# Host layouts for a two-block transformer kernel, with the second block's tokens grouped by residue mod 4

## The chip, the core and the metric

The kernel runs on one core of a Trainium2 chip. The metric is device time in microseconds (us) of one execution; a run's time is that of the core, and three runs of the kernel before gave a median of 3877.02 us. A core has TensorE (PE; its weight loads are shown apart as PEld), VectorE (DVE), ScalarE (ACT), GpSimd (POOL) and SyncE, whose queue (SP) issues every transfer of this kernel.

## What is computed

1024 tokens of width 1024 pass through two different transformer blocks, all in float32. The second block is applied twice (two layers). What matters here:

```python
# block 1
xn = rms_norm(x, norm_g);  proj = xn @ w_in        # q, k, v, z of both mixers
ya = rms_norm(diff_attention(q1, q2, k1, k2, va, lam, t5_bias)) * silu(za)
yb = neighbourhood_attention(qb, kb, vb, na_rpb) * silu(zb)
x  = x + concat(ya, yb) @ w_out
x  = x + sigmoid(x @ w_ple_gate) * (p @ w_ple_proj)
# block 2, two layers
h    = rms_norm(x, g) * (1 + sc1) + sh1;  proj = h @ w_in
o_dil = dilated_attention(q_d, k_d, v_d, positions, slopes)   # 8 heads
o_mla = latent_attention(...)                                 # dense, 8 heads
x = x + gt1 * (concat(o_dil, o_mla) @ w_out)
x = x + gt2 * (relu(h2 @ w_mlp_in) ** 2 @ w_mlp_out)
```

The dilated attention mixes three branches: a token attends to tokens t + j*dil with |j| <= 64 for dil = 1, 4 and 16 (the last covers the whole sequence at stride 16). For dil = 4 the tokens fall into four streams by their residue mod 4, and each stream is an attention among its own 256 tokens.

## The kernel before

A matrix in float32 is split into a rounded high part and the rest, and a product is three matmuls (`mm3`, L181 to L185: L183, L184, L185) of 128 rows by 256 or 512 columns. Activations lie with features on partitions and tokens along the free axis ("a00h" is feature tile 0, first half of the tokens, high part). The instructions of each engine are put in order by a scheduler that works on a model of the timeline, so an edit in one place can shift the order in others. PE, DVE, ACT, POOL and SP each run their own list in order.

**Start.** `load_x` (L331) loads x by rows in tiles of 128 tokens, transposes them on PE (64 transposes, L155), splits them with the norm's gain into a..h and a..l (ACT L130, DVE L131), copies the raw transposed x (DVE L345) and stores it to `xTd[0]`, and sums squares from the rows (ACT L350). Small vectors are brought onto partitions by `columns` (L164): load as rows, transpose on PE (L169), copy. `consts1` (L271) builds the table of the relative bias of the differential attention by matmul, through DRAM copies `t5d` and `t5s`; `consts2` (L316) builds a skewed copy `rpbs` of the neighbourhood bias in DRAM, eight transfers from DRAM to DRAM. `mod_start` (L930) brings `b_mod`, the norm gains and c.

**Block 1.** Four units of differential attention and four of neighbourhood attention follow; `start` in `diff_groups` (L500) loads the bias tile from `t5s` and `t5d`, `start` in `na_groups` (L615) loads `edge` from `rpbs` by two transfers of 64 partitions x 14 x 64 elements, and POOL adds a mask to it (L624). `put_mix` (L755) transposes an output to features on partitions. `ple_steps` (L359) loads p by rows and transposes it.

**Dilated stage.** For each of four pairs of heads, `stacks` (L424) transposes k and q, splits them and copies them by transfers into `ks0`, `ks1`, `qs0`, `qs1` (128 partitions x 1024 tokens: one head's high and low part); a half of the tokens at a time. `dil_groups` (L1299) then runs eight groups of scores per pair: for each head m first the near branch (x = 0), two groups of four query tiles, then the far branch (x = 1), two groups of four tiles. Each tile of scores is two matmuls (`score`, L459 with `ks`, L460 with `kl`) with 128 queries as weights and 256 keys as the moving operand. The far branch takes queries and keys of one residue by a stride of four tokens:

```python
# L1338, x == 1: stream cc, query tile u
q, ks = slice(cc + 512 * u, cc + 512 * u + 509, 4), slice(cc, cc + 1021, 4)
self.score(ps[:, k % 2, o:o + n], m, q, ks)
# L1369: the stream's output goes back with a stride of four
nc.scalar.copy(c["oTc"].rearrange("p (i c) -> p c i", c=4)[...], ...)
```

That makes 2 layers x 4 pairs x 2 heads x 2 groups x 4 tiles = 128 far tiles, and 128 near ones (96 of them 256 keys wide, in whole). DVE takes each tile from PSUM with a table of distances (`add_min`, L492 to L494), ACT applies the exponential (L1347), PE transposes and multiplies by v, which `scores` loads from DRAM: `v0` for the near branch, `v1` by four transfers for the far one.

**End.** In the last layer `mlp` (L1719) finishes with 16 products of 12 matmuls, each added to x on DVE (L1831); then `store_out` (L1889) transposes x back to rows on PE (64 transposes, L155), copies it out of PSUM (L1901, L1903) and stores it. The scheduler puts many of these transposes between the last products.

Of the kernel before, what the change touches and what calls it, by code (L numbers as in the profile page):

```python
# [15 lines left out]
OP = mybir.AluOpType  # L16
# [13 lines left out]


def shape_constants():
    rel = np.arange(-1023, 1024)
    n = np.abs(rel)
    large = 8 + np.searchsorted(np.array(T5_EDGES), n, side="right")
    bucket = np.where(rel > 0, 16, 0) + np.where(n < 8, n, np.minimum(large, 15))
    onehot = np.zeros((32, 2048), np.float32)
    onehot[bucket, np.arange(2047)] = 1.0
# [6 lines left out]
    wmask = np.where(np.abs(j - 64 - p) <= 64, 0.0, BIG).astype(np.float32)  # L45
# [7 lines left out]
    for cc in range(4):  # L53
        ec[np.arange(P), cc, cc + 4 * (np.arange(P) % 32)] = 1.0
    inv = np.float32(10000.0) ** (-np.arange(16, dtype=np.float32) / np.float32(16))
    return {"c_onehot": onehot, "c_colmask": colmask, "c_wmask": wmask, "c_cmult": cmult,
            "c_ec": np.concatenate([ec.reshape(P, 512), rmask], 1), "c_inv": inv.reshape(1, 16)}

# [28 lines left out]
class Emit:  # L87
# [76 lines left out]
    def columns(self, dst, src, n):  # L164
        nc = self.nc
        t = self.tmp.tile([P, P], F32, tag="colsrc", name="colsrc")
        self.dma(t[:n], src)
        ps = self.psum_t()
        nc.tensor.transpose(ps[:, :n], t[:n], self.ident[:n, :n])  # L169
        nc.vector.tensor_copy(dst, ps[:, :n])  # L170

# [61 lines left out]
    def setup(self):  # L233
# [23 lines left out]
        self.xTd = [self.dram.tile([8, P, S], F32, name=f"xTd{b}") for b in range(3)]  # L257
# [3 lines left out]
    def consts0(self):  # L261
        nc, A, c = self.nc, self.A, self.const
        self.gcol = c.tile([P, 8], F32, name="gcol")
        self.columns(self.gcol, A["norm_g"].rearrange("o (k p) -> (o k) p", p=P), 8)
        self.rs = c.tile([P, 8], F32, name="rs")
        self.hrs = c.tile([P, 8], F32, name="hrs")
        self.ev = c.tile([P, 8], F32, name="ev")
        self.xss = c.tile([P, 2, 8], F32, name="xss")
        self.xvar = c.tile([P, 8], F32, name="xvar")

    def consts1(self):  # L271
        nc, A, c = self.nc, self.A, self.const
        v = self.tmp.tile([P, P], F32, tag="colsrc", name="gsrc")
        for i, n in enumerate(("q_norm_a", "k_norm_a", "q_norm_b", "k_norm_b")):
            for j in range(2):
                self.dma(v[i:i + 1, j * 64:j * 64 + 64], A[n])
        ps = self.psum_t()
        nc.tensor.transpose(ps[:, :4], v[:4], self.ident[:4, :4])
        g4 = c.tile([P, 4], F32, name="g4")
        nc.vector.tensor_copy(g4, ps[:, :4])  # L280
        self.gq = c.tile([P, 2], F32, name="gqk")
        for i in range(2):
            nc.vector.scalar_tensor_tensor(self.gq[:, i:i + 1], g4[:, 2 * i:2 * i + 1], -0.125, g4[:, 2 * i + 1:2 * i + 2],
                                           op0=OP.mult, op1=OP.mult)
        tb = self.tmp.tile([32, 4], F32, name="t5b")
        self.dma(tb, A["t5_bias"])
        self.t5d = self.dram.tile([4, 2048], F32, name="t5d")
        for i in range(4):
            oh = self.tmp.tile([32, 512], F32, tag="onehot", name="onehot")
            self.dma(oh, A["c_onehot"][:, i * 512:(i + 1) * 512])  # L290
            row = self.tmp.tile([4, 512], F32, tag="t5row", name="t5row")
            ps = self.psum_t()
            nc.tensor.matmul(ps[:4], tb, oh, start=True, stop=True)
            nc.scalar.activation(row, ps[:4], AF.Copy, scale=-1.0)
            self.dma(self.t5d[:, i * 512:(i + 1) * 512], row)
        self.t5s = self.dram.tile([4, P, 520], F32, name="t5s")
        for i in range(4):
            t = self.t5s[i]
# [1667 lines left out]
```

## Time and profile before

| | |
|---|---|
| runs | 3874.85, 3877.02, 3882.91 us (median 3877.02) |
| profiled execution | 3880.11 us |
| its span, first to last instruction | 3878.2 us |
| mean granted TensorE clock | 0.973 of full speed |
| PE busy | 3613.2 us (93%) |
| PEld busy | 3097.2 us (80%) |
| DVE busy | 2821.6 us (73%) |
| ACT busy | 1842.2 us (48%) |
| POOL busy | 1565.9 us (40%) |
| chain that ended last | PE 59%, DVE 16%, POOL 8%, DMA 8%, issue 5%, ACT 4% |
| transfers | 446.17 MB, 36.7% of 16 DMA engines |

Busy times overlap across engines. A matmul's duration in the trace includes the filling and draining of the pipeline, so that matmuls overlap on PE; what one matmul costs is read from the time between its start and the start of the next one.

### The profile page before, as it was taken

Reading aid. Unit: us, or ns where it says so; the run is one execution under the profiler, and the core shown is the slowest. Engines: PE = TensorE matmul, PEld = TensorE weight load, DVE = VectorE, ACT = ScalarE, POOL = GpSimd, SP = SyncE. Lnnn points to the kernel's source line nnn. Section 1 sums busy time; section 2 is a strip of 40 time slices with the busy share of each in tenths; the row PEclk is TensorE's granted clock in tenths of the full one; section 3 lists DMA queues with packets and bytes.
Section 4 is the critical chain, followed back from the end, with each engine's and each line's share of the span. In section 5 each row is a group of like instructions: output and inputs, shape, how many; then the busy total and the mean of one; then the engine's idle time right before and its main releaser. Section 6 shows DMA issues by size and latency. Waiting matters only on the chain.

```text
span 3878.2 us, 59074 instructions
## 1 busy us (share of the span) xinstructions
PE 3613.2 (93%) x20508; PEld 3097.2 (80%) x20508; DVE 2821.6 (73%) x6304; ACT 1842.2 (48%) x3671; POOL 1565.9 (40%) x1317
## 2 busy tenths in 40 slices
PE   7999899989899899988998999899899998998999
PEld 6988899768899888777786777899788776886777
DVE  5888877667666788658889986666788646447885
ACT  4555555623455678533333333455677633333331
POOL 2334222322322223235337895422133235339882
PEclk9999999999899999999999999999999999999999
DMA  6322323575445500224555323455500132334322
GB/s 193 100 76 74 81 75 83 152 254 183 120 143 152 161 11 25 65 94 144 187 185 193 114 90 108 124 142 156 159 14 26 53 106 101 109 122 147 104 93 82
DMA packets 374077, 446.17 MB, mean 115 GB/s; under 512 B 50037, under 2 KB 246532, under 8 KB 373780
## 3 DMA queue, kind: packets, MB, share of 16 engines
q1 hardware_dynamic: 373780, 442.41, 36.7%
q8 instruction: 162, 2.65, 0.3%
q14 instruction: 135, 1.11, 0.1%
HBM read 312.17 MB, written 101.54 MB: 107 GB/s over the span
## 4 chain that ended last, share of the span: by engine, by line
PE 59%; DVE 16%; POOL 8%; DMA 8%; issue 5%; ACT 4%; SPq 1%; DVEq 0%; ACTq 0%; POOLq 0%
PE pg L183 8%; PE pg L184 8%; PE pg L185 8%; PE sps L1709 8%; PE pg L1709 6%; PE sps L459 2%; PE pt L155 2%; PE pt L693 2%; PE sps L460 2%; DVE macc L969 2%; PE sps L183 2%; DMA modraw<-in_w_mod_dram 2%; PE sps L184 2%; PE pa L700 2%; PE sps L185 2%
## 5 line engine op out<-in xcount | busy, mean ns | idle before, releaser
L209 POOL TENSOR_TENSOR wl<-raw,wh 128x512 fp32r<-128x512 f32 (+2 forms) x234 | 302.5, 1304 | 578.0 <-ACT wh L208 492.7
L128 DVE TENSOR_TENSOR pl<-pt,ph 128x512 fp32r<-128x512 f32 (+3 forms) x406 | 267.6, 665 | 85.8 <-ACT ph L127 77.3
L127 ACT CAST ph<-pt 128x512 fp32r<-128x512 f32 (+3 forms) x406 | 226.0, 574 | 136.1 <-PE pt L693 52.3
L208 ACT CAST wh<-raw 128x512 fp32r<-128x512 f32 (+2 forms) x234 | 138.1, 611 | 221.4 <-DMA raw<-in_w_out_dram 69.5
L969 DVE SCALAR_TENSOR_TENSOR macc<-modraw,csil,macc 128x256 f32<-128x256 f32 x280 | 205.3, 733 | 47.9 <-DMA modraw<-in_w_mod_dram 43.2
L459 PE MATMUL sps<-ks,qs 128*128 128x512 f32 (+3 forms) x480 | 195.8, 410 | 18.5 <-DVE mn L493 10.3
L1698 DVE TENSOR_TENSOR wl<-ssum,wh 128x1024 fp32r<-128x1024 f32 x116 | 168.6, 1453 | 47.5 <-ACT wh L1697 47.5
L1697 ACT CAST wh<-sraw 128x1024 fp32r<-128x1024 f32 x116 | 97.0, 836 | 221.8 <-PE sps L1709 121.4
L1684 POOL TENSOR_TENSOR ssum<-sraw 128x512 f32<-128x512 f32 x58 | 79.0, 1362 | 288.6 <-DVE wl L1698 122.7
L407 POOL TENSOR_TENSOR qn<-qn,r 128x512 f32<-128x512 f32 x64 | 68.8, 1080 | 266.5 <-DVE r L122 109.6
L460 PE MATMUL sps<-kl,qs 128*128 128x512 f32 (+3 forms) x480 | 175.4, 367 | 0.0
L1697 ACT CAST wh<-ssum 128x1024 fp32r<-128x1024 f32 x116 | 121.4, 1047 | 108.9 <-PE pg L1709 79.4
L1643 ACT ACTIVATE xm<-xm,mn 128x1024 f32<-128x1024 f32 x128 | 148.4, 1159 | 32.6 <-DVE mn L493 32.5
L493 DVE CUSTOM_DVE_ANT_0 xd<-sps,dtab 128x256 f32<-128x256 f32 (+1 forms) x256 | 103.3, 412 | 80.1 <-PE sps L460 72.0
L459 PEld LDWEIGHTS sps<-ks,qs 128*128 128x128 f32 x480 | 108.2, 225 | 28.5 <-DVE mn L493 15.0
L1698 POOL TENSOR_TENSOR wl<-sraw,wh 128x512 fp32r<-128x512 f32 x58 | 87.4, 1507 | 90.0 <-ACT wh L1697 81.4
L1698 DVE TENSOR_TENSOR wl<-sraw,wh 128x1024 fp32r<-128x1024 f32 x58 | 94.4, 1628 | 32.0 <-ACT wh L1697 23.9
L700 PE MATMUL pa<-pl,vpm 128*128 128x512 f32 x256 | 109.2, 427 | 2.9 <-DVE pl L128 2.7
L460 PEld LDWEIGHTS sps<-kl,qs 128*128 128x128 f32 x480 | 110.8, 231 | 1.3
L699 PE MATMUL pa<-ph,vpm 128*128 128x512 f32 x256 | 109.2, 427 | 0.6 <-ACT ph L127 0.2
L493 DVE CUSTOM_DVE_ANT_0 xm<-sps,zeros,mn 128x512 f32<-128x512 f32 x128 | 95.3, 745 | 13.8 <-PE sps L185 12.3
L693 PE MATMUL pt<-ident,xm 128*128 128x128 f32 x688 | 104.6, 272 | 0.6 <-DVE pl L128 0.6
(1483 smaller groups left out, 13960.6 us busy)
## 6 DMA issues: line engine op xcount, KB each, us to landing
modraw<-in_w_mod_dram SPq DMA_DIRECT2D x192, 256.0 KB
ud<-r SPq DMA_DIRECT2D x128, 256.0 KB
sraw<-in_w_mlp_in_dram SPq DMA_DIRECT2D x60, 512.0 KB
sraw<-in_w_mlp_out_dram SPq DMA_DIRECT2D x56, 512.0 KB
raw<-in_w_in_dram SPq DMA_DIRECT2D x194, 128.0 KB
uq<-ud SPq DMA_DIRECT2D x96, 256.0 KB
ks<-khh SPq DMA_DIRECT2D x128, 128.0 KB
dtab<-awd SPq DMA_DIRECT2D x32, 512.0 KB
```

The source lines that it names most:

```text
L127: nc.scalar.copy(hi, src)
L128: nc.vector.tensor_tensor(lo, src, hi.bitcast(F32), op=OP.subtract)
L183: nc.tensor.matmul(ps, lh, rh, start=start, stop=False)
L184: nc.tensor.matmul(ps, lh, rl, start=False, stop=False)
L185: nc.tensor.matmul(ps, ll, rh, start=False, stop=stop)
L209: nc.gpsimd.tensor_tensor(wl[:, sl], raw, wh[:, sl].bitcast(F32), op=OP.subtract)
L459: nc.tensor.matmul(ps, self.Q[m][:, q], self.K[m][:, k], start=True, stop=False)
L460: nc.tensor.matmul(ps, self.Q[m][:, q], self.KL[m][:, k], start=False, stop=True)
L969: nc.vector.scalar_tensor_tensor(acc, raw[:, k], c, acc, op0=OP.mult, op1=OP.add)
L1697: nc.scalar.copy(wh[:, 0:m], x)
L1698: (nc.vector if i < 3 else nc.gpsimd).tensor_tensor(wl[:, 0:m], x, wh[:, 0:m].bitcast(F32), op=OP.subtract)
L1709: nc.tensor.matmul(ps, x[:, k, cols], y, start=start and k + n == 0, stop=(k, n) == (nk - 1, 2), skip_group_check=True)
```

## The change

The host now hands over arrays in the layouts that the kernel needs, and takes the output back in another. `ORDER` lists the tokens of block 2: within each 64 tokens, the 16 of residue 0 first, then those of residue 1, 2 and 3. From block 1's residual on, the token axis is in that order; block 1's attention keeps the old order, and `put_mix` with b == 0 permutes its output.

```diff
+ORDER = np.arange(S).reshape(S // 64, 16, 4).transpose(0, 2, 1).reshape(S)
+def laid_out(A):
...
+    return {"x_t": np.asarray(A["x"])[0].T.reshape(8, P, S),
+            "x_o": np.asarray(A["x"])[0].T[:, ORDER].reshape(8, P, S),
+            "p_o": np.asarray(A["p"])[0, 0].T[:, ORDER].reshape(2, P, S),
...
+def stream(t):
+    return t.rearrange("p (b c j) -> p c b j", c=4, j=16)
...
     def load_x(self, a, g):
...
         for k in range(8):
-            ps = self.psum_t()
-            self.transposes(ps, [xs[t][:, k * P:(k + 1) * P] for t in range(4)])
+            x = self.tmp.tile([P, 512], F32, tag="x", name="xt")
+            self.dma(x, self.A["x_t"][k, :, g * 512:g * 512 + 512])
             hi, lo = self.act_tile(a, k, g)
-            self.split(hi, lo, ps, self.gcol[:, k:k + 1])
-            raw = self.up.tile([P, 512], F32, tag="w2k", name="xraw")
-            nc.vector.tensor_copy(raw, ps)
-            self.dma(self.xTd[0][k, :, g * 512:(g + 1) * 512], raw)
+            self.split(hi, lo, x, self.gcol[:, k:k + 1])
+    def x_stats(self, g):
+        rows = self.A["x"].rearrange("o s d -> (o s) d")
+        for t in range(4 * g, 4 * g + 4):
+            xt = self.tmp.tile([P, D], F32, tag="xr", name="xr")
+            self.dma(xt, rows[t * P:(t + 1) * P, :])
...
     def stacks(self, u, g, streams=False):
...
+            if streams:
+                for m, t in enumerate((qh, ql)):
+                    s = self.up.tile([P, 512], F32R, tag="hs", name="qstr")
+                    nc.gpsimd.tensor_copy(s.rearrange("p (c b j) -> p c b j", c=4, j=16), stream(t))
+                    for z in range(2):
+                        self.dma(self.QS[z][64 * (m ^ z):64 * (m ^ z) + 64, sl], s[64 * z:64 * z + 64])
...
-            for half in range(2):
-                rp = self.rpbs[h0 + m]
-                self.dma(edge[half * 64:half * 64 + 64],
-                         bass.AP(tensor=rp.tensor, offset=rp.offset + (1 - half) * 128 + 63, ap=[[1920, 64], [128, 14], [1, 64]]))
-            nc.gpsimd.tensor_tensor(edge, edge, self.colmask.unsqueeze(1).to_broadcast([P, 14, 64]), op=OP.add)
+            self.dma(edge.rearrange("p s k -> p (s k)"), self.A["rpb"][h0 + m])
+            nc.gpsimd.tensor_tensor(edge, self.colmask.unsqueeze(1).to_broadcast([P, 14, 64]), edge, op=OP.subtract)
...
-                        self.dma(vw[:, 2 * cc:2 * cc + 2], rows.rearrange("(u p c) d -> c p u d", c=4, p=P)[cc][:, :, hd])
+                        for u in range(2):
+                            self.dma(vw[:, 2 * cc + u], rows.rearrange("(u b c j) d -> u c b j d", u=2, c=4, j=16)[u, cc][:, :, hd])
...
-                    q, ks = slice(cc + 512 * u, cc + 512 * u + 509, 4), slice(cc, cc + 1021, 4)
+                    q, ks, kl = self.QS[m][:, 512 * u + cc * P:512 * u + cc * P + P], stream(K)[:, cc], stream(KL)[:, cc]
...
-                nc.scalar.copy(c["oTc"].rearrange("p (i c) -> p c i", c=4)[:, 2 * b:2 * b + 2, :], ops.rearrange("p (c i) -> p c i", c=2))
+                nc.scalar.copy(stream(c["oTc"])[:, 2 * b:2 * b + 2], ops.rearrange("p (c b j) -> p c b j", c=2, j=16))
...
-                    if l == 0:
-                        self.dma(self.xTd[2][d, :, half * 512:half * 512 + 512], self.X(d, half))
+                    self.dma((self.out if l else self.xTd[2])[d, :, half * 512:half * 512 + 512], self.X(d, half))
...
-            self.store_out()
```

The rest, in words: `columns` and all its uses go (gains, c and b_mod come in one packed array and two small ones); the bias tables of both attentions come ready from the host (`t5`, one transfer per unit and a negation on ACT; `rpb`, one transfer of 128 x 896 per head), so that the DRAM copies `t5d`, `t5s` and `rpbs` go; p comes transposed; `out_proj` of block 1 reads x from `x_o` where `xTd[0]` was; the masks, the position table and the selection matrix of `dil_merge` follow the new order.

The scheduler moves instructions. Three places, as the lists of the engines have them:

PE, the first group of the far branch in layer 0 (`ks`, `kl` are the keys' high and low stacks, `qs` the query stack, `qss` the new one; `pg` is the next pair's projection, `pa` the near branch's product with v), before:

```order
L183 MATMUL pg<-wh,a51h 128x256
L459 MATMUL sps<-ks_12880,qs_12878 128x256
L460 MATMUL sps<-kl_12338,qs_12878 128x256
L184 MATMUL pg<-wl,a51h 128x256
L1388 MATMUL pa<-ph,v_12936 128x256
L459 MATMUL sps<-ks_12880,qs_12878 128x256
L460 MATMUL sps<-kl_12338,qs_12878 128x256
L185 MATMUL pg<-wh,a51l 128x256
```

and now:

```order
L208 MATMUL pg<-wh,a51h 128x256
L1316 MATMUL sps<-ks_12609,qss_12069 128x256
L1317 MATMUL sps<-kl_12065,qss_12069 128x256
L209 MATMUL pg<-wl,a51h 128x256
L1364 MATMUL pa<-ph,v_12681 128x256
L1316 MATMUL sps<-ks_12609,qss_12069 128x256
L1317 MATMUL sps<-kl_12065,qss_12069 128x256
L210 MATMUL pg<-wh,a51l 128x256
```

The order is the same here; the query operand is the new stack.

SP, the transfers of the first pair's stacks, second half of the tokens, and the loads of v behind them (`khh`, `qhh`, `qll` are the split k and q; `v_12936` serves the near branch, `v_13187` the far one), before:

```order
L108 DMA ks_12881<-khh 64x512 x2
L108 DMA qs_12878<-qhh 64x512
L108 DMA qs_12878<-qll 64x512
L108 DMA qs_12879<-qhh 64x512
L108 DMA qs_12879<-qll 64x512
L108 DMA v_12936<-vd 64x128
L108 DMA v_12936<-vd 128x7x128
L108 DMA v_13187<-vd 128x2x128 x4
```

and now (`qstr` is the query regrouped on POOL):

```order
L141 DMA ks_12610<-khh 64x512 x2
L141 DMA qs_12607<-qhh 64x512
L141 DMA qs_12607<-qll 64x512
L141 DMA qs_12608<-qhh 64x512
L141 DMA qs_12608<-qll 64x512
L141 DMA qss_12069<-qstr 64x512
L141 DMA qss_12070<-qstr 64x512
L141 DMA qss_12069<-qstr 64x512
L141 DMA qss_12070<-qstr 64x512
L141 DMA v_12681<-vd 64x128
L141 DMA v_12681<-vd 128x7x128
L141 DMA v_12932<-vd 128x1x128 x4
```

Four transfers of `qss` per half stand behind the `qs` ones and ahead of the loads of v, and the far branch's v comes in smaller transfers.

SP, the first transfers of the program, before:

```order
L108 DMA colsrc<-in_norm_g_dram 8x128
L108 DMA xt<-in_x_dram 128x1024 x4
L108 DMA raw<-in_w_in_dram 128x2x128 x4
L108 DMA gsrc<-in_q_norm_a_dram 1x64 x2
L108 DMA gsrc<-in_k_norm_a_dram 1x64 x2
```

and now:

```order
L141 DMA pack<-in_pack_dram 128x163
L141 DMA raw<-in_w_in_dram 128x2x128 x4
L141 DMA xt<-in_x_t_dram 128x512 x4
L141 DMA xr<-in_x_dram 128x1024
L141 DMA raw<-in_w_in_dram 128x2x128 x4
L141 DMA xt<-in_x_t_dram 128x512 x4
L141 DMA xr<-in_x_dram 128x1024 x3
```

The weights `raw` now go ahead of x, x comes feature by feature (`xt`), and the rows for the squares (`xr`) come between.

## Rows read from the trace of the kernel before

**Rows 1.** Windows: start, dilated stage of each layer, end; PE, PEld, DVE, ACT, POOL, clock, DMA.
```profile
0.00:104.00 104.00, 83.86 (x567) 74.75 (x568) 52.58 (x164) 45.02 (x97) 28.73 (x32) 0.93 0.65 190
1020.00:1300.00 280.00, 274.63 (x2003) 259.75 (x2002) 180.43 (x617) 147.72 (x379) 61.33 (x72) 0.99 0.55 160
2580.00:2780.00 200.00, 195.67 (x1372) 181.28 (x1371) 135.30 (x469) 115.73 (x302) 39.23 (x52) 1.00 0.58 173
3838.00:3878.20 40.20, 35.28 (x181) 28.87 (x180) 13.22 (x19) 4.30 (x8) 0.00 (x0) 0.98 0.28 105
```
**Rows 2.** Timeline, first far pair: start us, duration us, engine, line, out<-in.
```profile
1060.09 0.31 PEld L459 LDWEIGHTS sps<-ks,qs 128*128 128x128 f32 x1
1060.21 0.49 PE L459 MATMUL sps<-ks,qs 128*128 128x256 f32 x1
...
1060.30 0.33 PEld L460 LDWEIGHTS sps<-kl,qs 128*128 128x128 f32 x1
1060.52 0.42 PE L460 MATMUL sps<-kl,qs 128*128 128x256 f32 x1
...
1060.75 0.30 PE L184 MATMUL pg<-wl,a51h 128*128 128x256 f32 x1
```
**Rows 3.** Timeline, last far pair of layer 1: its start and the next one's.
```profile
2785.28 0.58 PE L459 MATMUL sps<-ks,qs 128*128 128x256 f32 x1
...
2785.91 0.42 PE L459 MATMUL sps<-ks,qs 128*128 128x256 f32 x1
```
**Rows 4.** Timeline, a near pair in layer 0.
```profile
1125.05 0.28 PE L459 MATMUL sps<-ks,qs 128*128 128x256 f32 x1
1125.06 0.19 PEld L460 LDWEIGHTS sps<-kl,qs 128*128 128x128 f32 x1
1125.17 0.28 PE L460 MATMUL sps<-kl,qs 128*128 128x256 f32 x1
...
1125.29 0.28 PE L183 MATMUL pg<-wh,a61h 128*128 128x256 f32 x1
```
**Rows 5.** Waits of PE in 0 to 110 us: waited for, us in total, times, longest.
```profile
PE pt L169 <- DMA colsrc<-in_b_mod_dram: 5.9, 1, 5.9
...
PE pt L155 <- DMA xt<-in_x_dram: 3.1, 4, 1.2
```
**Rows 6.** Timeline of PE at 12 us: four early transposes, and the wait ahead.
```profile
12.44 1.08 PE L155 MATMUL pt<-ident,xt 128*128 128x128 f32 x4 [2.11 <-DVE xvar L353]
```
**Rows 7.** Chain of waits at 3842 us: four transposes.
```profile
3842.44 0.44 PE pt L155 x4
```
**Rows 8.** Timeline at the end: the last five stores, last product, its addition.
```profile
3869.44 5.45 SPq L108 DMA_DIRECT2D out_dram<-oo  x5
...
3870.84 0.39 PE L185 MATMUL pg<-a11h,wl 128*128 128x512 f32 x1
...
3871.28 0.75 DVE L1831 SCALAR_TENSOR_TENSOR b23l<-pg,mod,b23l 128x512 f32<-128x512 f32 x1 [1.86 <-PE pg L185]
```
**Rows 9.** Timeline at the first neighbourhood unit: the bias load, POOL, PE.
```profile
461.86 3.47 SPq L108 DMA_DIRECT2D edge<-rpbs  x4
...
467.19 2.08 POOL L624 TENSOR_TENSOR edge<-edge,colmask 128x896 f32<-128x896 f32 x1 [13.03 <-DMA edge<-rpbs]
...
473.96 0.64 PE L459 MATMUL sps<-ks,qs 128*128 128x320 f32 x1 [5.67 <-DVE mn L493]
```
**Rows 10.** Timeline at 469 us: a copy on POOL.
```profile
469.33 0.72 POOL L626 COPY inner<-edge 128x640 f32<-128x640 f32 x1
```
**Rows 11.** Timeline at 101 us: four issues on SP.
```profile
100.86 2.38 SPq L108 DMA_DIRECT2D ks<-khh  x4
```
**Rows 12.** Chain of waits at 14 us: the landing of a 128 KB transfer.
```profile
14.65 4.75 DMA raw<-in_w_in_dram
```
**Rows 13.** Waits of PE in 2580 to 2780 us, the longest.
```profile
PE sps L459 <- DMA qs<-qhh: 1.4, 1, 1.4
```
**Rows 14.** Waits of POOL in 1020 to 1300 us, the longest.
```profile
POOL v L1316 <- PE pa L1389: 51.8, 4, 30.1
```

More of the change, by code (lines that the diff above doesn't have):

```diff
@@ L256, in setup @@
         self.mixd = [self.dram.tile([8, P, S], F32, name=f"mixd{b}") for b in range(3)]
-        self.xTd = [self.dram.tile([8, P, S], F32, name=f"xTd{b}") for b in range(3)]
+        self.xTd = [self.A["x_o"]] + [self.dram.tile([8, P, S], F32, name=f"xTd{b}") for b in (1, 2)]
         self.xTm = self.dram.tile([8, P, S], F32, name="xTm")
@@ L261, in consts0 @@
     def consts0(self):
-        nc, A, c = self.nc, self.A, self.const
-        self.gcol = c.tile([P, 8], F32, name="gcol")
-        self.columns(self.gcol, A["norm_g"].rearrange("o (k p) -> (o k) p", p=P), 8)
+        c = self.const
+        pk = self.pk = c.tile([P, 163], F32, name="pack")
+        self.dma(pk, self.A["pack"])
+        self.gcol, self.ct, self.g4, self.gsub = pk[:, 0:8], pk[:, 8:16], pk[:, 16:20], pk[:, 20:21]
         self.rs = c.tile([P, 8], F32, name="rs")
@@ L272, in consts1 @@
         nc, A, c = self.nc, self.A, self.const
[L273 to L280, printed above, removed]
         self.gq = c.tile([P, 2], F32, name="gqk")
         for i in range(2):
-            nc.vector.scalar_tensor_tensor(self.gq[:, i:i + 1], g4[:, 2 * i:2 * i + 1], -0.125, g4[:, 2 * i + 1:2 * i + 2],
+            nc.vector.scalar_tensor_tensor(self.gq[:, i:i + 1], self.g4[:, 2 * i:2 * i + 1], -0.125, self.g4[:, 2 * i + 1:2 * i + 2],
                                            op0=OP.mult, op1=OP.mult)
[L285 to L298, printed above, removed]
-            self.dma(bass.AP(tensor=t.tensor, offset=t.offset, ap=[[513, P], [1, 512]]),
-                     self.t5d[i:i + 1, 768:1280].to_broadcast([P, 512]))
         lam = self.tmp.tile([P, 4, 64], F32, name="lam")
-        for i, n in enumerate(("lam_q1", "lam_k1", "lam_q2", "lam_k2")):
-            self.dma(lam[:, i, :], A[n].to_broadcast([P, 64]))
+        self.dma(lam.rearrange("p a b -> p (a b)"), A["lams"])
         ls = c.tile([P, 4], F32, name="lams")
@@ L368, in act @@
         def act(half):
-            raw = self.up.tile([P, 4, 256], F32, tag="z", name="pz")
-            self.dma(raw, self.A["p"][0, 0, half * 512:half * 512 + 512].rearrange("(t p) e -> p t e", p=P))
+            raw = self.up.tile([P, 2, 512], F32, tag="z", name="pz")
+            self.dma(raw, self.A["p_o"][:, :, half * 512:half * 512 + 512].rearrange("k p s -> p k s"))
             hl = self.up.tile([P, 2, 2, 512], F32R, tag="vp", name="pvp")
             for k in range(2):
-                ps = self.psum_t()
-                self.transposes(ps, [raw[:, t, k * P:(k + 1) * P] for t in range(4)])
-                self.split(hl[:, k, 0], hl[:, k, 1], ps, 0.5)
+                self.split(hl[:, k, 0], hl[:, k, 1], raw[:, k], 0.5)
             s["p"] = hl
@@ L931, in mod_start @@
         nc, A, c = self.nc, self.A, self.const
-        ct = c.tile([P, 8], F32, name="ct")
-        self.columns(ct, A["c_2"].rearrange("o (k p) -> (o k) p", p=P), 8)
+        ct = self.ct
         th = c.tile([P, 8], F32, name="cth")
@@ L1460, in dilated @@
         self.open_keys()
+        self.QS = [self.up.tile([P, S], F32R, tag=f"qss{m}", name=f"qss{m}") for m in range(2)]
         self.ec = self.ap.tile([P, 516], F32, name="ec")
@@ L1964 @@
     r = run_bass_kernel_spmd(nc, [arrays], core_ids=[0])
-    return r.results[0]["out_0_dram"]
+    y = np.empty((1, S, D), np.float32)
+    y[0, ORDER] = r.results[0]["out_0_dram"].reshape(D, S).T
+    return y
```

172 lines of the change are left out of this document (66 added, 106 removed).

## The prediction

> **What bounds the kernel now.** I read four views in this order: the windows by stage, the waits of PE inside a stage, the timeline of single instructions, and the chain of waits at both ends. In the windows [rows 1] the reader should set PE's busy time beside each length. In the dilated stages it is 274.6 of 280 us and 195.7 of 200, with DVE at 64 to 68%, ACT at 53 to 58% and the DMA engines at 55 to 58%: these stages are paced by PE, and the granted clock is 0.99 to 1.00, so time comes out of them only if PE has less to do. The start (83.9 of 104 us, clock 0.93, DMA 0.65) is different: 20 us of it are idle PE. The end (35.3 of 40.2) lies between.
>
> So the questions are what a far tile of scores costs on PE, what stands on the path at both ends, and whether the added transfers stay covered. The sum is made against the profiled execution of 3880.11 us (span 3878.2); the median of the runs, 3877.02, is 3.1 lower, and I take the 3.1 off at the end. About 0.2%, 8 us, is what a measurement of this kernel can tell from no change.
>
> **A. Far scores.** What one matmul costs is the time to the next start. The first far pair starts at 1060.21, its second matmul at 1060.52 and the next instruction at 1060.75: 0.54 us [rows 2]. The last far pair takes 0.63 [rows 3]. A near pair of the same size takes 0.24 [rows 4]. The weight loads differ too: 0.31 and 0.33 us for far queries [rows 2], 0.19 for near ones [rows 4]. Queries and keys of a far tile are both read with a stride of four float32 values. Now the queries come contiguous from the new stack, so the weight load should look like the near one. The keys are read in runs of 16 values with gaps of 48; no row of the trace shows that access, so it is bounded. If only the jump inside a run matters, the pair costs 0.24 as the near one. If keys stay at half speed, as a stride reads them now, each matmul costs twice 0.12 and the pair 0.48. A price below 0.24 is excluded, since the near pair is already contiguous on both sides. I take 0.24, because 15 of 16 steps are the near pair's steps. The gain is 0.54 - 0.24 = 0.30 us, by 128 pairs 38 us, and about nine tenths of it lies on PE's path (its waits in these stages are about 2% of their length, but the scheduler's order is not the same everywhere): **34 us**. With the dear keys, 0.06 x 128 = 8, taken as 9 because the last pair was dearer.
>
> The Trainium skill (SBUF — State Buffer, section Door 1: The DMA port swizzle, its note on cachelines) says that full bandwidth wants at least two hits in each 16-byte line, which is four float32 values; a stride of four hits each line once, a run of 16 hits each line four times. The trace agrees on the stride (0.54 against 0.24); for runs of 16 the page would give the near price, and no row shows it yet.
>
> **B. Start.** On PE go 64 transposes of x, which cost 0.11 each (four take 0.44 us [rows 7]; the early ones 1.08 for four [rows 6]): 7.0 us. About 13 small matmuls of the old constants go: 1.4. Three waits go with them: 5.9 for `b_mod` by rows, 3.1 for x [rows 5] and 2.1 for the sum of squares ahead of a transpose [rows 6], together 11.1. Sum 19.5. Against it: x is now read twice, once by features for the product and once by rows for the squares, while the store of the transposed x and the DRAM copies of the two bias tables go; and the second half of `xt` stands on SP behind weights and one row tile, as the excerpt of SP's first transfers shows. One 128 KB transfer lands 4.75 us after its issue at this point [rows 12]. I take **17 us**; the bounds are 0 (the stage is paced by transfers and PE waits instead) and 28 (all the idle 20 us and the 8.4 of work).
>
> **C. End.** 64 transposes go. About 48 of them stand between the last products: 48 x 0.11 = 5.3. Behind the last product, at 3870.84, there are now transposes, copies and stores; the issues end at 3869.44 + 5.45 = 3874.89, and the span 3.3 later [rows 8]. In the change the addition (3871.28 + 0.75 = 3872.0) is followed by one issue of about 0.4 and a landing of 3.3: 3875.7, so 2.5 earlier. Together **8 us**; bounds 5.3 (the tail is as long) and 13 (the idle 4.9 goes as well).
>
> **D. p and small edits.** 16 transposes of p: 16 x 0.11 = **2**. The copies to `oTc`, the permuted read in `put_mix`, the negation of the bias and the packed constants are on ACT, DVE or SP beside PE's work; ACT is busy for 53 to 58% of the dilated stages [rows 1]. I cost them at nothing; uncovered, the `oTc` copies alone would be 32 x 1.1 us (an estimate from a 0.72 us POOL copy of 640 columns [rows 10]). They become cheaper, not dearer.
>
> **E. Neighbourhood bias.** PE waits 5.67 us at the first such unit behind a load in pieces of 256 bytes; POOL's addition waits for it [rows 9]. One contiguous transfer takes its place: **2**, of 0 to 5.7.
>
> **F. What is added.** 32 regrouping copies on POOL (0.72 each [rows 10]), 64 `qss` transfers and 64 more for v, the issues on SP at 2.38 per four [rows 11]: 128 x 0.6 = 77 us of queue time, spread over 480 us of dilated stages. They are covered by the near branch, which runs first in each pair. Should they be late, the first far tile of a pair is late next, and v behind it on SP. At pair boundaries I charge **2 us**; bounds 0 and what rivals 2 and 4 say.
>
> Sum: 34 + 17 + 8 + 2 + 2 - 2 = 61. 3880.1 - 61 = 3819, against the median **3816 us**.
>
> **Rivals.**
>
> 1. *Key reads stay slow.* The jump of 256 bytes could cost as the stride does now. For it: no row shows runs. Against: far weight loads are slower than near ones by themselves [rows 2, 4], so the far pair's price need not come from the keys at all. Gain 9 in place of 34: 3816 + 25 = **3841**. Chance 0.12.
>
> 2. *The freed PE time turns into waits.* In 16 halves of stacks (2 layers, 4 pairs, 2 halves) DVE, ACT or a load ends last instead. For it: the longest wait of PE in layer 1's window is already one for `qs`, 1.4 us [rows 13]. Against: every other engine is below 70% [rows 1]. 34/16 = 2.1 us each takes the whole of A: **3850**. Chance 0.11.
>
> 3. *The start is paced by transfers.* DMA is 0.65 busy there [rows 1] and x comes twice. B gives nothing: 3816 + 17 = **3833**. Chance 0.12.
>
> 4. *Slower: the regrouping chain is exposed.* Per half it is two POOL copies (1.44), four issues (2.38) and a landing (4.75): 8.6 us. POOL takes its list in order and has waited 30.1 us at one instruction in this stage [rows 14]; a copy behind such a wait is late, and `qss` with it. Fully exposed: 16 x 8.6 = 137 instead of 2, 3816 + 135 = **3951**. It decides from 63/16 = 3.9 us per half. Against it: the near branch runs first, and a pair has about 70 us (four pairs in the 280 us of [rows 1]). Chance 0.04.
>
> 5. *Slower: the loads of v come late.* They go from 4 transfers to 8 for a head's far branch, each in shorter pieces. If each head waits for one more landing of 4.75 [rows 12], 16 x 4.75 = 76: **3892**. For it: `v` stands last in SP's excerpt. Against: a head has some 35 us. Chance 0.02. The Trainium skill (DMA: Bandwidth & Descriptors, section Why a DMA increments its semaphore by 16 and not by 1) lets a transfer use as many engines, up to 16, as divide the slowest dimensions of both sides; with 8 in the source of the new load that would be 8 in place of 16, and no run here shows it.
>
> **How the numbers follow.** Forecast 0.59; the rivals have 0.41. Low end: the whole 38 of A (4 more), 28 of B (11), 13 of C (5), 5.7 of E (4) and nothing for F (2) would be 26 below: 3790. High end: 3850, which holds rivals 1 to 3. Left out are rivals 4 and 5 (0.06) and an order of the scheduler that is worse or better than I can see. Faster by over 0.2% are the forecast and rivals 1 to 3, less a little for mixtures: 0.93. Within 0.2%: 0.02. Slower: 0.05, rivals 4 and 5.
>
> **What would show it.** A: far pairs 0.24 us apart and far weight loads at 0.19; at 0.48 rival 1 holds. A shorter dilated window with the same PE idle time supports A; a busy PE that falls while the length stays is rival 2. B: the first differential scores some 17 us earlier, the three waits gone; PE waiting for `xt` or `raw` instead is rival 3. C: one store and its landing after the last addition. F: no wait on `qss` above 1 us. The prediction is wrong if the dilated stages are less than 15 us shorter together, or if PE waits for POOL's `qstr` there.

## The result and the profile after

The change takes 3817.47 us (median of four runs, 3815.55 to 3819.93); on the same chip the kernel before takes 3876.1 us. The ratio is 0.9846, with a 95% interval of 0.9828 to 0.9863. The forecast was 3816 us. The profiled execution has a span of 3818.2 us against 3878.2 before: 60.0 us less.

The total came out as forecast. To see whether its parts did, the same instructions of the two traces were matched by name and order (how much earlier one starts in the other trace is called its lead); the bounds of the windows below stand at such matched instructions. First the windows of the kernel before at the places that the change's windows answer to (columns as in [rows 1]):

```profile
975.00:1310.00 335.00, 316.95 (x2252) 297.65 (x2251) 225.47 (x726) 174.59 (x432) 80.86 (x91) 0.96 0.51 151
2450.00:2830.00 380.00, 353.17 (x2520) 331.53 (x2521) 261.08 (x859) 210.43 (x538) 90.18 (x106) 0.96 0.47 139
```

The windows of the changed kernel: start, dilated stage of each layer, end.

```profile
0.00:104.00 104.00, 84.54 (x611) 80.40 (x612) 67.20 (x217) 56.02 (x117) 38.98 (x40) 0.95 0.53 162
950.00:1277.50 327.50, 305.24 (x2282) 286.56 (x2282) 223.61 (x731) 169.26 (x434) 91.63 (x105) 0.96 0.56 164
2408.50:2780.00 371.50, 340.38 (x2520) 316.61 (x2521) 257.23 (x847) 201.10 (x539) 103.92 (x124) 0.94 0.54 156
3778.00:3818.20 40.20, 36.43 (x161) 29.84 (x159) 10.51 (x14) 0.00 (x0) 0.00 (x0) 1.00 0.26 98
```

The dilated stages are 7.5 and 8.5 us shorter. PE is busy 12 to 13 us less in each, so part of what PE was spared did not become time. All of the 60 us, by the lead of matched instructions:

| stretch of the kernel before | lead at its end | gained in it | forecast |
|---|---|---|---|
| 0 to 950 us (start, block 1, p) | 25.1 | 25.1 | 17 + 2 + 2 |
| 950 to 1350 (dilated, layer 0) | 32.5 | 7.4 | 16 (half of 34 - 2) |
| 1350 to 2400 (layer 0's rest, MLP) | 40.9 | 8.4 | 0 |
| 2400 to 2850 (dilated, layer 1) | 50.5 | 9.6 | 16 |
| 2850 to 3878 (layer 1's rest, end) | 60.0 | 9.5 | 8 |

A far pair of scores did become a near one. The timeline of the changed kernel at the pair that answers to [rows 2]:

```profile
1034.69 0.29 PE L1316 MATMUL sps<-ks,qss 128*128 128x256 f32 x1
1034.82 0.28 PE L1317 MATMUL sps<-kl,qss 128*128 128x256 f32 x1
1034.94 0.28 PE L209 MATMUL pg<-wl,a51h 128*128 128x256 f32 x1
```

1034.69 to 1034.94 is 0.25 us where it was 0.54. Over 112 far pairs with nothing waited for behind them, the mean is 0.289 us (0.159 and 0.130); in the kernel before it is 0.558 over 120.

The end, with the last product, its addition and the one store behind it:

```profile
3814.04 0.39 PE L210 MATMUL pg<-a11h,wl 128*128 128x512 f32 x1
3814.47 0.75 DVE L1808 SCALAR_TENSOR_TENSOR b23l<-pg,mod,b23l 128x512 f32<-128x512 f32 x1 [1.97 <-PE pg L210]
3815.25 0.33 SPq L141 DMA_DIRECT2D out_dram<-b23l  x1
```

From the last product's start to the end of the span it is 4.2 us (3818.2 - 3814.04), against 7.4 before (3878.2 - 3870.84, [rows 8]).

So the experiments ask four things: what the reads alone are worth, what the second stack costs, what gave the start its 25 us, and where 8.4 us in the MLP of layer 0 come from. They ran on other chips, where the kernel before takes 3882 to 3886 us in the median; ratios are compared, not times. One caution comes from them: before, e1 and e7 run identical programs up to 950 us, and their profiled executions differ there by up to 11 us (leads of 0, -6.1 and -10.9). From 950 to 1800, again the same in before and e7, the lead stayed within 1.5; but layer 1's dilated stage, the same in the change and in e8, differs by 3.0. A difference of 3 us in a stage shows nothing.

### The profile page after: what moved, and what is told of

Read it like the earlier page. It is cut to its first block, busy times and chain, and to the rows that moved or that the text cites. A ratio compares the mean times of both kernels' runs of the same rounds, so it can differ in the third digit from the quotient of the medians.

```text
span 3818.2 us, 58767 instructions
## 1 busy us (share of the span) xinstructions
PE 3552.9 (93%) x20344; PEld 3044.0 (80%) x20344; DVE 2790.6 (73%) x6264; ACT 1814.7 (48%) x3663; POOL 1585.5 (42%) x1349
## 4 chain that ended last, share of the span: by engine, by line
PE 52%; DVE 9%; POOL 9%; DMA 6%; issue 4%; ACT 3%; SPq 0%; POOLq 0%; DVEq 0%; ACTq 0%
PE sps L1686 9%; PE pg L1686 7%; PE pg L208 6%; PE pg L210 6%; PE pg L209 6%; PE pt L677 2%; PE sps L208 2%; PE sps L209 2%; PE sps L210 2%; POOL uq L1789 1%; PE pt L188 1%; PE pa L684 1%; PE pa L683 1%; DMA sraw<-in_w_mlp_out_dram 1%; DMA uq<-ud 1%
## 5 line engine op out<-in xcount | busy, mean ns | idle before, releaser
L1674 ACT CAST wh<-ssum 128x1024 fp32r<-128x1024 f32 x116 | 121.4, 1047 | 103.8 <-PE pg L1686 77.3
L448 PE MATMUL sps<-ks,qs 128*128 128x512 f32 (+1 forms) x224 | 92.2, 412 | 22.1 <-DVE mn L482 16.3
L161 DVE TENSOR_TENSOR pl<-pj,ph 128x512 fp32r<-128x512 f32 (+2 forms) x138 | 90.1, 653 | 29.0 <-ACT ph L160 24.5
L524 ACT ACTIVATE x<-x,mn 128x1024 f32<-128x1024 f32 x64 | 73.9, 1154 | 76.6 <-DVE mn L482 70.9
L1704 ACT COPY keep<-sps 128x512 f32<-128x512 f32 x60 | 35.2, 587 | 143.4 <-PE sps L1686 143.3
```

The costliest lines, as they stand in the source:

```text
L161: nc.vector.tensor_tensor(lo, src, hi.bitcast(F32), op=OP.subtract)
L1674: nc.scalar.copy(wh[:, 0:m], x)
```

## The experiments

### e1: the reads alone, in the kernel before

```diff
-                self.score(ps[:, k % 2, o:o + n], m, q, ks)
+                if x == 0:
+                    self.score(ps[:, k % 2, o:o + n], m, q, ks)
+                else:
+                    q = self.Q[m][:, 512 * u + cc * P:512 * u + cc * P + P]
+                    for i, t in enumerate((self.K[m], self.KL[m])):
+                        t = t.rearrange("p (b c j) -> p c b j", c=4, j=16)[:, cc]
+                        nc.tensor.matmul(ps[:, k % 2, o:o + n], q, t, start=i == 0, stop=i == 1)
```

> The kernel before, with the far branch's queries read contiguously from the stack it has and its keys in runs of 16, as in the change; no copy or transfer is added, the far scores are of the wrong tokens. Far pairs should be about 0.29 us apart instead of 0.57, 36 us less PE time over 128 pairs. Theory 1 (half of the freed PE time is not on the path: it turns into waits of PE and dearer neighbours in the dilated stages): about 17 us faster, 3859 us. Theory 2 (the prediction's nine tenths hold for the reads alone, and the other half was taken by the added copies and transfers): about 34 us faster, 3842 us.

Measured: ratio 0.9942 (0.9922 to 0.9961), 15 to 30 us, middle 22. The lead grows by 11 us in layer 0's dilated stage and by about 13 in layer 1's. The window of layer 1, at the same instructions as 2450 to 2830 before:

```profile
2446.60:2813.00 366.40, 339.37 (x2520) 314.94 (x2521) 259.60 (x859) 209.00 (x538) 90.10 (x106) 0.95 0.50 144
```

PE is busy 13.8 us less and the window is 13.6 us shorter. Theory 1's 17 us lie within the interval of the runs, theory 2's 34 outside it; the two stages give 24. So the reads give more than half of the 36 us, and they give it one for one with PE's busy time.

### e2, e4, e5: a stride back in the changed kernel

The edits, shortened:

```diff
-q, ks, kl = self.QS[m][:, 512*u + cc*P:512*u + cc*P + P], stream(K)[:, cc], stream(KL)[:, cc]
+q = self.QS[m][:, cc + 512*u:cc + 512*u + 509:4]      # e2, e5
+ks, kl = K[:, cc:cc + 1021:4], KL[:, cc:cc + 1021:4]  # e2, e4
```

> The changed kernel, with the far branch's queries and keys read with a stride of four again (wrong tokens; the new stack is still made). Theory 1: about 17 us slower than the changed kernel, 3834 us, although PE spends 36 us more on far pairs. Theory 2: the reads alone are worth 34, 3851 us. Rival on the keys: if only an unlucky order in the dilated stages hid the gain, anything over 20 us.

> The changed kernel with only the keys of the far branch read with a stride of four; the queries stay contiguous (wrong tokens). If the moving operand's stride makes the far pair dear: 0.45 us or more per pair and a time near that of the kernel with both strided. If the strided weights alone do: 0.29 us per pair and the changed kernel's time, 3817 us. Theory 1 expects that whatever the pair costs, about half of the PE time shows in the end.

> The changed kernel with only the far queries (the weights) read with a stride of four, from the new stack (wrong tokens); keys in runs of 16. With keys alone strided the kernel was about 12 us slower than the changed one, with both about 28 to 31. If the two operands' prices add up: far pairs near 0.43 us and 15 us slower, about 3832 us on a chip where the changed kernel takes 3817. If a pair's price is the larger of the two (weights load under the matmul before): the same as both strided, far pairs 0.55 us and 28 us slower.

The order of the instructions is the same in the changed kernel and in e2, so that the reads are the only difference. Groups by line, first of the changed kernel (busy us, mean ns of one | idle before):

```profile
L1317 PEld LDWEIGHTS sps<-kl,qss 128*128 128x128 f32 x128 | 24.3, 190 | 0.1
L1316 PE MATMUL sps<-ks,qss 128*128 128x256 f32 x128 | 39.9, 321 | 5.0 <-DVE mn L482 4.9
```

of e2 (both strided):

```profile
L1317 PEld LDWEIGHTS sps<-kl,qss 128*128 128x128 f32 x128 | 42.2, 330 | 0.0
L1316 PE MATMUL sps<-ks,qss 128*128 128x256 f32 x128 | 64.4, 503 | 0.2
```

of e4 (keys strided):

```profile
L1317 PEld LDWEIGHTS sps<-kl,qss 128*128 128x128 f32 x128 | 25.4, 199 | 0.9
L1316 PE MATMUL sps<-ks,qss 128*128 128x256 f32 x128 | 55.4, 433 | 1.8 <-DVE mn L482 1.8
```

and of e5 (queries strided):

```profile
L1317 PEld LDWEIGHTS sps<-kl,qss 128*128 128x128 f32 x128 | 42.2, 330 | 0.0
L1316 PE MATMUL sps<-ks,qss 128*128 128x256 f32 x128 | 55.3, 432 | 2.2 <-DVE mn L482 2.2
```

The weight load takes 330 ns for strided queries whatever the keys do, and 190 to 199 for contiguous ones.

| | far pair | ratio to before | lead lost in the two dilated stages |
|---|---|---|---|
| change | 0.289 us | 0.9846 (0.9828 to 0.9863) | - |
| e4, keys strided | 0.486 | 0.9872 (0.9847 to 0.9897) | 10 + 5 |
| e5, queries strided | 0.511 | 0.9889 (0.9864 to 0.9915) | 13 + 9 |
| e2, both strided | 0.564 | 0.9918 (0.9899 to 0.9937) | 13.4 + 13.5 |

Either stride alone takes the pair most of the way: the two prices, 0.20 and 0.22 us, do not add up to the 0.275 of both. From both strided, freeing the queries alone (e4) saves 0.078 us a pair and 12 us of the 27, freeing the keys alone (e5) 0.053 and 5. These shares rest on one execution each, and that of e5 was the slowest of its four; by the runs the intervals of e4 and e5 overlap.

In e2 PE spends 0.275 x 128 = 35 us more on far pairs and the two stages are 27 us longer: 77% is on the path. The lines above show most of the rest: before the first matmul of far scores PE is idle for 5.0 us in the change, 4.9 of them until DVE has taken an earlier tile of scores (`mn`), and for 0.2 us in e2. The 27 us are 10 off theory 1's 17 and 7 off theory 2's 34; by the runs, e2 is 28 us slower than the change, give or take 10, which leaves out 17 barely and 34 not at all, and it is e1 that leaves out 34. The third branch of the expectation (over 20 us: an unlucky order of the instructions hid the gain) is met as well, and no run separates the order.

The forecast's dear keys (0.48 a pair) were the right price for strided keys; runs of 16 values are not strided in that sense: the pair costs 0.289, and a near pair in the changed kernel 0.263 in layer 0 and 0.285 in layer 1. The note on cachelines of the Trainium skill (SBUF — State Buffer, section Door 1: The DMA port swizzle), by which four float32 values of a line read one after the other go at full bandwidth, agrees with both: 0.486 against 0.289.

### e3, e11, e12: what the second stack costs

e3 makes no `qss` at all; e11 writes the high parts straight into it; e12 moves the copies to ACT (the edits of e11 and e12, shortened):

```diff
 # e11, in the loop over (qh, ql)
+                    if m == 0:
+                        for z in range(2):
+                            h = slice(64 * z, 64 * z + 64)
+                            nc.gpsimd.tensor_copy(self.QS[z][h, sl].rearrange("p (c b j) -> p c b j", c=4, j=16), stream(t[h]))
+                        continue
 # e12
-                    nc.gpsimd.tensor_copy(s.rearrange(...), stream(t))
+                    nc.scalar.copy(s.rearrange(...), stream(t))
```

> The changed kernel without the second query stack: no regrouping copies on POOL, no transfers of it; the far queries are read contiguously from the first stack (wrong tokens). Theory 1: within 4 us of the changed kernel, 3814 to 3821. Theory 2: some 17 us faster, 3800 us. The prediction charged 2 us for these copies and transfers.

> The changed kernel; the high parts of the regrouped queries are written by POOL straight into the second stack, on the partitions that they have already, so that 32 of its 64 transfers go; POOL makes 48 copies instead of 32. Taking all copies and transfers away made the dilated stages about 8 us shorter. If the transfers and SP's issues cost that: 2 to 4 us faster than the changed kernel. If POOL's time does: 2 to 4 us slower.

> The changed kernel with the 32 regrouping copies on ACT instead of POOL. If POOL's list (copies queued behind its waits, and its normalisation of q behind the copies) is what the second stack costs: up to 8 us faster. If ACT's exponentials are what PE waits for, or the transfers cost it: within 3 us, or slower.

| | ratio to before | dilated stages against the change |
|---|---|---|
| e3 | 0.9828 (0.9808 to 0.9848) | 1 + 5 us shorter |
| e11 | 0.9829 (0.9813 to 0.9845) | 6 + 5 us shorter |
| e12 | 0.9863 (0.9849 to 0.9877) | 7 + 1 us longer |

Over the whole program e3 and e11 are 0.17 to 0.18% below the change, 7 us, and their intervals overlap with its own; inside the stages the traces show 6 and 11 us, and a stage with the same instructions differs by up to 3. That lies between the two theories, 4 us and 17; a cost of 6 to 11 is likely. e11 took 3818.88 us in the median (3809.47 to 3827.71) on a chip 10 us slower for the kernel before; that it beats the change is likely, not shown.

Where the stack costs is a boundary between pairs of heads. PE's waits at one of them, before (2548 to 2590 us):

```profile
PE pa L1366 <- DVE pl L128: 1.1, 2, 0.8
PE pt L155 <- DVE qll L131: 1.0, 1, 1.0
PE pg L183 <- ACT qn L396: 0.7, 1, 0.7
PE pt L155 <- DVE kl L437: 0.3, 1, 0.3
```

in the change (2505 to 2535):

```profile
PE pg L208 <- ACT qn L379: 2.7, 1, 2.7
PE pt L188 <- DVE qll L164: 1.7, 1, 1.7
PE pt L188 <- DVE kl L420: 1.5, 2, 1.3
```

and in e11 (2505 to 2535):

```profile
PE pt L188 <- DVE kl L420: 2.3, 1, 2.3
PE pg L208 <- ACT qn L379: 0.7, 1, 0.7
```

The waits on the three steps that make the next stacks (`qn`, `qll`, `kl`) go from 2.0 to 5.9 us in the change; in e11 they are 3.4 (with 0.4 on `qll`). Over both dilated stages PE's waits on these steps and on the transfers of `ks` and `qs` are 7 us before and in e1, 14 in the change and in e2, 8 in e3, 6 in e11 and 15 in e12. So they come with the stack, or with the order that it brings, and not with the cheaper reads: e2 has the stack and the dear reads.

The chain of waits of the change, between 2505 and 2535 us, names what holds PE at this boundary:

```profile
2520.39 4.52 DMA ks<-khh
2525.13 0.59 ACT khh L417
```

The split of k for the second half of the tokens (`khh`) takes the buffer of the first half's, three buffers serving three splits a half, and waits 3.6 us for the first half's transfers to `ks`; `kl` on DVE and `qn` on ACT come behind it. Before, the two splits stand at 2566.8 and 2571.9 us and neither waits. The `qss` transfers of the first half are issued at 2524.07, behind these `ks` transfers (2518.58), so on SP they do not hold them up here.

The windows of 20 us around the boundary, before and in the change, show a second price (the eighth column is the granted clock):

```profile
2550.00:2570.00 20.00, 18.02 (x124) 16.70 (x122) 14.24 (x57) 11.89 (x34) 0.40 (x2) 1.00 0.41 124
2570.00:2590.00 20.00, 18.56 (x144) 18.33 (x145) 13.05 (x48) 8.72 (x21) 4.33 (x5) 0.91 0.56 144
```

```profile
2510.00:2530.00 20.00, 14.01 (x96) 12.63 (x95) 13.69 (x42) 11.59 (x30) 4.78 (x8) 0.79 0.70 180
2530.00:2550.00 20.00, 20.00 (x167) 20.00 (x166) 14.52 (x58) 9.75 (x28) 5.50 (x7) 0.95 0.50 137
```

PE is idle for 6 of 20 us, with the clock at 0.79 and then 0.95 (2.4 GHz in part, 1.2 in part), against 0.91 before. The stretch at 1.2 GHz lies inside these windows:

```profile
2521.60:2531.80 10.20, 6.42 (x28) 5.76 (x28) 3.81 (x6) 2.73 (x5) 4.38 (x6) 0.50 0.95 212
```

Of its 10.2 us PE works 6.4, which at the full clock would take about half (an estimate): some 3 us lost, against some 2 at the 0.91 before. In e11 the same place has a clock of 0.91. So an idle PE at a boundary can be paid for twice.

Moving the copies off POOL does not help (e12), and more of them on POOL do not hurt (e11 makes 48 and is shorter in both stages); but ACT also makes `qn`, so e12 alone does not clear POOL. e11 has half the transfers, which would speak for them, and yet at the boundary shown it is the transfers of `ks` that are waited for. e3 and e11 have other orders of the instructions than the change, too: whether the copies and transfers cost the 6 to 11 us, or the order that the scheduler makes with them, is not shown.

### e6: x by rows again

```diff
         for k in range(8):
-            x = self.tmp.tile([P, 512], F32, tag="x", name="xt")
-            self.dma(x, self.A["x_t"][k, :, g * 512:g * 512 + 512])
+            ps = self.psum_t()
+            self.transposes(ps, [xs[t][:, k * P:(k + 1) * P] for t in range(4)])
...
-            self.x_stats(0)
```

> The changed kernel with x loaded by rows once and transposed on PE as before (64 transposes, squares from the same rows); no store of the transposed x, and all other layouts as in the change. By the prediction's own terms this is worth 7.0 us of transposes and 5.2 us of waits: about 12 us slower, half of the 25 that the start gained. Rival: x by features gains nothing, since x is read twice and the start is paced by transfers, and the whole 25 come from the constants and tables: within 3 us.

Measured: ratio 0.9837 (0.9820 to 0.9854), the change's time. Its lead on the change, counted by the matmul work that both share, is 0.8 us at 100 us and 0.7 at 950. PE's longest wait in the first 110 us is now

```profile
PE pt L188 <- DMA xt<-in_x_dram: 9.4, 4, 8.1
```

where the change waits

```profile
PE pg L208 <- ACT a00h L163: 7.7, 1, 7.7
```

64 transposes more, x read once instead of twice, and nothing lost: by 100 us both stand at the same place. The rival holds for x; of the constants and tables e6 says nothing.

### e9, e10: the constants, in the kernel before

```diff
-        for h in range(8):                     # e9, e10
-            t = self.rpbs[h]
-            self.dma(bass.AP(tensor=t.tensor, ...), rpbd[h:h + 1].to_broadcast([64, 1920]))
...
-                rp = self.rpbs[h0 + m]
+                rp = self.A["w_in"][0][128 * (h0 + m):128 * (h0 + m) + 128]
...
-            self.columns(m, A["b_mod_2"][l].rearrange("(k p) -> k p", p=P), 48)   # e10
+            self.dma(m, A["b_mod_2"][l].rearrange("(p k) -> p k", p=P))
```

The reason for them is in the chain of waits of the kernel before, between 42 and 82 us (start, us, what):

```profile
42.14 6.72 DMA rpbs<-rpbd
48.88 10.23 DMA rpbs<-rpbd
...
67.89 1.73 DMA t5d<-t5row
...
72.13 9.63 DMA colsrc<-in_b_mod_dram
```

28 of these 40 us are constants' transfers; x has none.

> The kernel before without the eight transfers that build the skewed bias copy in DRAM; the loads of the neighbourhood bias read other data in the same pattern (wrong bias). In the chain of waits of before these transfers hold 17 us between 42 and 59 us. If they pace the start: 10 to 17 us faster by 110 us, about 3865 us where before takes 3877. If they only stand in the chain because nothing behind them was urgent: under 4 us faster.

> As the kernel without the skewed copy, and besides the two modulation biases are loaded directly instead of by rows and a transpose on PE (wrong values). PE's wait of 5.9 us for these rows goes. If the constants are what gave the start its 25 us: together 18 to 25 us faster than before, about 3855 us, with x still loaded by rows and transposed. If x by features had its part: at most 10.

e9: ratio 0.9930 (0.9919 to 0.9942), 27 us faster, more than either branch of its expectation. Its first scores come 10.5 us earlier (93.3 against 103.8), but other work of PE comes later for it: counted by the matmul work that both kernels share, e9 is level with the kernel before at 150 us (0.3), 8 us ahead at 200, 13.5 at 500 and 16.5 at 950; at the end of the profiled execution it is 20. By the caution above, the stretch before 950 us is known to some 11 us; the 27 us of the runs do not hang on it. Some 5 of the 20 lie far from the start, in layer 0's MLP (see e7).

e10: ratio 0.9976 (0.9966 to 0.9986), 9 us faster, where 18 to 25 were expected if the constants are the cause and at most 10 if x has a part, which e6 contradicts. By the same count it is 3.7 us ahead at 150 us, 2.6 at 450 and 1 behind at 950. In e10 PE waits for the next rows of that kind instead:

```profile
PE pt L169 <- DMA colsrc<-in_g_norm_mix_dram: 4.5, 1, 4.5
```

So taking the skewed copy out of the kernel before gains 27 us by itself, and taking one column load away only uncovers the next. Why e10, which lacks the skewed copy as well, falls behind e9 is open: the scheduler gives the two kernels other orders, and no run separates that. Nor is it shown that the skewed copy is what gave the change its start: by the same count the change and e6 are 18 us ahead at 110 us, where e9 is 0.6 ahead and e10 3.5. Which of the edits left (the other column loads, the table built through `t5d` and `t5s`, the weights ahead of x) gave these 18 us was not tested.

### e7: the rotation of PSUM buffers

```diff
         gt = self.mod[l][:, 40:48]
+        if l == 0:
+            self.turn += 1
```

> The kernel before with the rotation of the transposes' PSUM buffers moved on by one at the MLP of layer 0, and nothing else; the result is the reference's. In the trace of before two modulation pieces in layer 0's MLP, at 1865 and 1947 us, take the buffer pj and make PE wait about 2 us each, and at just these two places the changed kernel gains 3.4 and 3.7 us. If the phase of the rotation is the cause: some 7 us less between 1840 and 1960 us, and both waits gone. If the changed layouts themselves are the cause: no difference there.

The same three transposes of modulation pieces in the timelines of the kernel before,

```profile
1850.56 0.38 PE L155 MATMUL pt<-ident,macc 128*128 128x128 f32 x2
...
1865.14 0.41 PE L155 MATMUL pj<-ident,macc 128*128 128x128 f32 x2 [2.14 <-DVE macc L969]
...
1963.59 0.38 PE L155 MATMUL pt<-ident,macc 128*128 128x128 f32 x2
```

of e7,

```profile
1862.81 0.38 PE L155 MATMUL pj<-ident,macc 128*128 128x128 f32 x2
1875.10 0.38 PE L155 MATMUL pt<-ident,macc 128*128 128x128 f32 x2
...
1967.90 0.38 PE L155 MATMUL pt<-ident,macc 128*128 128x128 f32 x2
```

and of the change:

```profile
1817.85 0.38 PE L188 MATMUL pj<-ident,macc 128*128 128x128 f32 x2
...
1830.63 0.41 PE L188 MATMUL pt<-ident,macc 128*128 128x128 f32 x2 [0.35 <-DVE macc L957]
...
1923.34 0.38 PE L188 MATMUL pt<-ident,macc 128*128 128x128 f32 x2
```

First to last takes 113.0 us before, 105.1 in e7 and 105.5 in the change. Every third transposed group goes to `pj`; the piece at 1865 us hits it before and waits 2.14 us for DVE, the one at 1947 us waits 1.97, and with the count moved by one nobody waits there. Each wait is paid for twice here, too: right behind the first, PE is busy throughout, at half the clock,

```profile
1865.90:1869.20 3.30, 3.30 (x9) 2.59 (x8) 3.23 (x9) 0.00 (x0) 0.00 (x0) 0.50 0.77 235
```

and so it is from 1947.8 to 1951.2 us; 2 us of wait and half of 3.4 are about the 3.4 and 3.7 us that the change gains at the two places. In e7 and in the change the clock does not fall there. The layouts are not needed for the 7.5 us: a moved count is enough.

But the count does not settle it alone. e9 has the same instructions on PE and DVE in this stretch as the kernel before, with `pj` at the same pieces, and takes 107.2 us: the piece that answers to 1865 us waits,

```profile
1854.43 0.41 PE L155 MATMUL pj<-ident,macc 128*128 128x128 f32 x2 [1.97 <-DVE macc L965]
```

the clock stays at 1.00, and the one that answers to 1947 us does not wait. The other trace with that phase, e1, takes 112.7. With the other phases ten traces take 104.9 to 106.2 us and one, e5, 109.4 with a wait of 2.1. So the old phase goes with longer stretches, but executions with one phase differ by up to 6 us, and what decides whether a wait comes is not shown.

Moved on for the rest of the program too, the count gives back 3 us by 2060 and more later: e7 as a whole is no faster (1.0012, 1.0001 to 1.0022).

### e8: rows out

```diff
-                    self.dma((self.out if l else self.xTd[2])[d, :, half * 512:half * 512 + 512], self.X(d, half))
+                    if l == 0:
+                        self.dma(self.xTd[2][d, :, half * 512:half * 512 + 512], self.X(d, half))
...
+            self.store_out()
```

> The changed kernel with the output transposed back on PE and stored by rows at the end, as before. The prediction's term C: 8 us slower, 5.3 of it between the last products and 2.5 behind them. The two traces give 9 to 10 from the last products to the end, so 8 to 10 us slower; the rest of the program does not change.

Ratio 0.9861 (0.9833 to 0.9888), 6 us slower than the change, with intervals that overlap. Matched to the change, e8 has lost 3.8 us by 3700 us, where the two programs are the same, and 13.4 by the end: 9.6 for the output. From its last product, at 3824.40 us, to the end of its span it takes 7.2 us against 4.2.

## Why the prediction was right, and which of its terms were not

The total (3816 against 3817.5) is better than its parts, and that is luck. By the working:

- **A, 34 us: the price was right, the share on the path too high.** A far pair costs 0.289 instead of the 0.24 taken, and 0.564 instead of 0.54 with strides, so PE is spared 35 us, near the 38. "About nine tenths of it lies on PE's path" failed: e2 shows 27 us, 77%, with PE waiting for DVE in place of most of the rest; e1, in the order of the kernel before, shows some 24. The nine tenths were read from windows in which PE is busy for 98% of the time; the whole stages before, boundaries included, have 95 and 93%. A slip without effect: the pair called the last [rows 3] is the last but one; the last starts at 2785.91 and takes 0.48 us.
- **F, 2 us: mis-sized.** Between the 27 us of the reads (e2) and the 17 of the two stages lie 10 for all that the change adds there: the stack, smaller loads of v, another order. e3 shows 6 and e11 11 for the stack or its order. Rival 2 (freed time turned into waits) had the place right and the reason in part: the waits on the steps that make the stacks double with the stack, also where the reads stay dear (e2), and in e1, with the cheap reads and no stack, they stay and the stages shorten by 24 us, not 17. The waits for DVE under A are of rival 2's kind.
- **B, D and E, 21 us: 25 measured, but not for the reason given.** The seven microseconds of x transposes and the waits for x were worth nothing (e6). The chain of waits names constants instead: the skewed copy of the bias in DRAM, for which B charged nothing, and which E touched only where it is read, is worth 13.5 us by 500 us to the kernel before (e9). How much of it the change got so is not shown, and what put the change 18 us ahead by 110 us stays open. B read the waits of PE, and an engine's wait names what came last for it, not what would be last next.
- **C, 8 us: 9.5.** 3.2 behind the last product (2.5 forecast), the rest between the products (e8: 9.6).
- **Not forecast: 7.5 us** in layer 0's MLP, from waits that a moved rotation of PSUM buffers takes away (e7), though one execution with the old rotation lost most of them as well (e9); the whole program shows no such gain by itself.

The misses are -7, -8, +4, +1.5 and +7.5 us: -2 in sum. The range was met because they have both signs. The sign of being wrong that was named for A, dilated stages less than 15 us shorter together, was missed by one us (16), within the scatter of a stage. Of the rivals, 1 is refuted by 0.289 us; 3 holds in that x gains nothing, but not in its sum; 4 and 5 did not come: in the dilated stages PE waits for no transfer of `qss` and for no load of v. That a load of v uses fewer engines there, as the Trainium skill (DMA: Bandwidth & Descriptors, section Why a DMA increments its semaphore by 16 and not by 1) would have it, no run shows; if it does, the cover of a head was enough.

## What to carry to other kernels

Before a matmul operand is costed, look at both accesses: a strided weight load and a strided moving operand each cost most of the price of both here, so that mending one alone buys less than half. Read the share of freed PE time that will show from the whole stage, boundaries between groups included (here three quarters of it showed); at a boundary a few microseconds of idle PE were followed by a lower clock, too. For a start with idle PE, read the chain of waits first and ask of each removed wait what is late next; removing the work that the engine's waits name may give nothing.

## What was not expected of the hardware

- A stride of four float32 values costs on both sides: 330 against 190 ns for a weight load, and 0.486 against 0.289 us for a pair with strided keys; runs of 16 values with gaps of 48 hardly do (0.289, near pairs 0.263 and 0.285).
- The phase of a rotation that sends every third group of transposes to another PSUM buffer is worth 7.9 us in 113 (e7), at two places: at each, 2 us of wait and then 3.4 us at half the clock. The same order and phase took 107.2 us in another execution (e9).
- Eight transfers from DRAM to DRAM, which nothing needs before the neighbourhood units, hold 17 us of the chain at the start, and the program is 27 us shorter without them (e9), of which little shows before 180 us.
